# The first stream's matrix memory turned by VectorE blocks and DRAM, in the second stream's written order

## The chip, the cores and the metric

The kernel runs on one core of one Trainium2 chip. The metric is the device time of one execution in microseconds (us). A core has five engines that run their own instruction queues: TensorE (PE; its weight loads are shown as PEld), VectorE (DVE), ScalarE (ACT), GpSimd (POOL) and SyncE (SP), the last of which issues most of the DMAs here.

## The reference

One encoder layer on two independent sequences of 512 tokens and 1024 channels, called stream 0 (the prompt) and stream 1 (the sample). Cut to what matters:

```python
x = x + 0.5 * swiglu(rms_norm(x, ffn1_norm), ...)
h = rms_norm(x, mix_norm)
aq, ak, av, mq, mk, mv, gate_pre, o_pre, g_att, g_mlstm = split(h @ w_in)
att = gqa_block_attention(rope(norm(aq)), rope(norm(ak)), av)         # 8 heads of 64
mem = mlstm_bidirectional(mq, mk, mv, gate_pre, bias, o_pre, head_norm)  # 4 heads of 128
merged = sigmoid(g_att) * (att @ w_up_att) + sigmoid(g_mlstm) * (mem @ w_up_mlstm)
x = x + merged @ w_out
x = x + 0.5 * swiglu(rms_norm(x, ffn2_norm), ...)
```

The matrix memory `mlstm_bidirectional` is written chunk by chunk, forward and backward. It equals, for each head, a 512x512 matrix of scores q·k times exponential weights (a lower triangle for the forward direction, an upper one for the backward direction), each row divided by its own denominator, times the values. Then come an RMS norm over each head, a gain and a sigmoid gate.

## The kernel before

**Tiling.** Activations are held transposed, channels on the 128 partitions and 512 tokens along the free axis, as a pair of float32r tiles: a rounded part (hi, `xh`) and the rest (lo, `xl`). Every weight is split in the same way, on ScalarE (hi, L284) and VectorE (lo, L285), and every product takes three matmuls (hi·hi, hi·lo, lo·hi). Stream 0 reads raw weights from the inputs, splits them and parks both parts in DRAM (L309); stream 1 reads them back (L299).

**Order.** The body is written with a tile framework whose planner puts the instructions of each engine into a queue: it simulates the program, takes the ready instruction of the highest priority (program order, changed by `shifted(n)`), and gives each tile a place in its pool when it is first touched; a place comes free with the last use of its tile. `pin` keeps one instruction behind the one written before it on its engine, and `mark` does so where `marks[0]` is set. So the written order is a preference, and on the chip the queues are fixed.

**Units.** `go` (L792) takes units (load, compute). It calls a unit's load at once and keeps `ahead[0]` units waiting in `held` (1 in stream 0, 2 in stream 1) before it writes their matmuls. In stream 0 the load (`load_w`, L292) reads the raw weights, splits them and parks them. A projection unit has 24 matmuls of 512 columns (8 blocks of 128 channels, three products), an `up_unit` (the merges) 12.

**Pools.** `apool` has seven places of 16 KB a partition (line 31: `bufs=7`, all under one tag): xh, xl, box, kv, qT, mg, att, mem, Vm, mh, ml and others take turns in them. `wpool` has four places `wr` for raw weights and four `w8` for split ones; `t2` has eleven tiles of 128x512 and `f2` four.

**The matrix memory.** `mix(s, ...)` runs for each stream s. After attention it does four heads:

- `mem_head(h)` (L1299): four blocks of scores (L1309, three matmuls each), the exponential weights on ScalarE (L1323), their product with row sums on VectorE (L1325), the denominators (L1329 to L1331), and one row of 512 weights for each 128 queries (L1336 to L1339). The masked rows come from `mem_rows` (L1091), on VectorE in stream 1 and for head 0, on GpSimd for heads 1 to 3 of stream 0.
- In stream 0, `mem_out(h, Ts)` (L1359) turns these 512x512 weights by 16 TensorE transposes of 128x128 (L1372), splits each turned piece from PSUM (L733, L734) and multiplies with the values `Vm` (L1381).
- In stream 1, `mem_blocks` (L1342) turns 32x32 blocks on VectorE (eight instructions a head, L1347) into two `wr` tiles, `mem_send` (L1351) writes them to DRAM with eight DMAs of GpSimd's queue, and `mem_out` reads each piece back whole with a DMA (L1368). The product comes out with its tokens in block order, and a copy (L1387) puts it right.
- Both end with the norm and the gate of the head and a split into `mem[:, h]`.

Other units fill TensorE meanwhile: values, the queries and keys of later heads (`mem_qk`), attention gates, `merge_att` (needs `att`), input gates `mem_gate`. `merge_mem` (L856 into the banks pss and pst) needs all four heads. Stream 1 has its order written out by hand, with sends of one head ahead of the product of the head before (L1401); stream 0 runs a loop of four heads with a queue of fillers (L1423).

Of the kernel before, what the change touches and what calls it, by code (L numbers as in the profile page):

```python
# [16 lines left out]
P = 128  # L17
# [9 lines left out]
def encoder(ctx, tc, I, outs):  # L27
# [91 lines left out]
    def f(ap):  # L119
        return ap.bitcast(F32)  # L120
# [171 lines left out]
    def load_w(view, key, park=True):  # L292


        if key in parked:
            d, shape = parked[key]
            w2 = wpool.tile(shape, F32R, tag="w8", bufs=4, name=nm("w"))
            for i in range(2):
                nc.sync.dma_start(f(w2[:, i]), d[:, i])  # L299
            return w2[:, 0], w2[:, 1]  # L300
        raw = fetch_w(view)
        with shifted(-WEIGHTS):
            hi, lo = split_w(raw, V_)
        if not park:
            return hi, lo
        shape = [P, 2] + list(raw.shape[1:])
        parked[key] = d, _ = dpool.tile(shape, F32, name=nm("wpark")), shape
        for i, t in enumerate((hi, lo)):
            nc.sync.dma_start(d[:, i], f(t))  # L309
        return hi, lo  # L310

# [470 lines left out]
    win_v = w_in.rearrange("(k p) c -> p k c", p=P)  # L782


    held = []
    ahead = [1]
    marks = [False]

    def mark(i, last):
# [1 line left out]

    def go(*units):  # L792
        for load, comp in units:
            held.append((comp, load()))
            while len(held) > ahead[0]:
                c, w = held.pop(0)
                c(w)

    def flush():
        while held:  # L800
            c, w = held.pop(0)
            c(w)

# [61 lines left out]
    def mix(s, xh, xl, early=None, extra=None, after=None):  # L865
# [9 lines left out]
        def F2(dtype=F32):  # L875
            return T2(dtype, "f2")
# [207 lines left out]
        def mem_rows(h, d):  # L1084

            eb = T2(F32, "eb")
            eb3 = eb.rearrange("p (b s) -> p b s", b=4)
            nc.sync.dma_start(eb3, ebuf[d, :, h, :].partition_broadcast(P))
            em = T2(F32, "eb")
            em3 = em.rearrange("p (b s) -> p b s", b=4)  # L1090
            (V_ if s or not h else G_).tensor_tensor(em3, eb3, tabs[3][:, d].unsqueeze(1).to_broadcast([P, 4, P]), op=ALU.add)  # L1091
            return eb3, em3

        def mem_scales():
# [91 lines left out]
        def among(n):  # L1186
            for _ in range(n):
                if not between:
                    if not held:
                        return  # L1190
                    c, w = held.pop(0)
                    if queue:
                        load, c2 = queue.pop(0)
                        held.append((c2, load()))
                    between.extend(c.steps(w))
                between.pop(0)()

# [62 lines left out]
        def up_unit(part, d, src, done, bank=None):  # L1260
            def load():
                if d % 2 == 0:
                    wv = I[("w_up_att", "w_up_mlstm")[part]][0].rearrange("(k p) c -> p k c", p=P)
                    wups[part, d // 2] = load_w(wv[:, :, d * P:(d + 2) * P], ("up", part, d))

            def comp(_):
                wu = wups[part, d // 2]
                cl = slice((d % 2) * P, (d % 2 + 1) * P)
                done(proj_w(wu[0][:, :, cl], wu[1][:, :, cl], lambda k: (src[:, k, 0, :], src[:, k, 1, :]), 4,
                            bank and bank()))  # L1270
            return load, comp

        def merge_att(d):
            def done(pu):
                V_.scalar_tensor_tensor(mg[:, d, :], mg[:, d, :], 1.0, pu, op0=ALU.add, op1=ALU.mult)
            return up_unit(0, d, att, done)
# [64 lines left out]

        def mem_blocks(h, Ts):  # L1342

            q = [wpool.tile([P, 8, 4, 32], F32, tag="wr", bufs=4, name=nm("qt")) for _ in range(2)]
            for i in range(4):
                for g in range(2):
                    V_.transpose(q[g][:, :, i, :],  # L1347
                                 Ts[i][0][:, g * 256:(g + 1) * 256].rearrange("p (n m) -> p n m", m=32))
            return h, q

        def mem_send(h, q):  # L1351

            for g in range(2):
                for a in range(4):
                    mark(nc.gpsimd.dma_start(tbuf[h % 2][8 * g:8 * g + 8, :, a, :].rearrange("n r x -> r n x"),
                                      q[g][32 * a:32 * a + 32].rearrange("r n i m -> r n (i m)")), True)
            return h % 2

        def mem_out(h, Ts):  # L1359
# [32 lines left out]
            turned_ = own[0] if own else F2()  # L1392
            row = block_sums(h2, turned_)
            with shifted(60):
                rh = block_rstd(row, DM)
# [2 lines left out]
                V_.scalar_tensor_tensor(og, og, hn[:, h:h + 1], Rh, op0=ALU.mult, op1=ALU.mult)  # L1398
                split(og, mem[:, h, 0, :], mem[:, h, 1, :])

        if s:  # L1401
            qk2, qk3 = [[mem_qk(h, j) for j in range(2)] for h in (2, 3)]
            ma = [merge_att(d) for d in range(KD)]
            marks[0] = True
            q = mem_blocks(0, mem_head(0))
            at = [mem_send(*q)]
            go(*mem_values(), *qk2)
            q = mem_blocks(1, mem_head(1))
            go(*qk3, ma[0], ma[1])
            mem_out(0, at[0])  # L1410
            at.append(mem_send(*q))
            q = mem_blocks(2, mem_head(2))
            go(att_gate(6), att_gate(7), ma[2], ma[3])
            mem_out(1, at[1])
            at.append(mem_send(*q))
            q = mem_blocks(3, mem_head(3))
            go(*ma[4:])
            mem_out(2, at[2])
            at.append(mem_send(*q))
            go(*[mem_gate(d) for d in range(EARLY)])  # L1420
            mem_out(3, at[3])
            marks[0] = False
        for h in range(HM if not s else 0):  # L1423
            Ts = mem_head(h)
            if h == 0:
                go(*mem_values())
            queue.append(merge_att(2 * h))
            if h == 0:
                queue.append(merge_att(1))
            fill(1 + s)  # L1430
            mem_out(h, Ts)
            if h + 2 < HM:
                queue.extend([att_gate(h + 6), mem_qk(h + 2, 0), mem_qk(h + 2, 1)])
            if h:
                queue.append(merge_att(2 * h + 1))
            fill(99)
# [4 lines left out]
        flush()  # L1441
        yield None


# [551 lines left out]
```

## Time and profile before

| | us |
|---|---|
| median of 3 runs | 2030.96 |
| the runs | 2028.93 to 2032.43 |
| the profiled execution | 2029.24 |
| its span, first to last instruction | 2027.5 |

| stage of the profiled execution | us from the span's start |
|---|---|
| first feed-forward block, both streams | 0 to 649 |
| stream 0: projections and attention | 649 to 811 |
| stream 0: matrix memory, from its first score | 797 to 930 |
| stream 0: merges with memory | 955 to 977 |
| stream 1: projections and attention | 977 to 1185 |
| stream 1: matrix memory | 1168 to 1310 |
| second feed-forward block | 1382 to 2027 |

In the profile's rows an L number is a line of the kernel. A row of groups gives the number of instructions, their busy time, the mean length of one, and the idle time of the engine just before them with what ended it. A row of windows gives, for a stretch of time, the busy time of PE, PEld, DVE, ACT and POOL with the number of instructions, then TensorE's granted clock and the busy share and rate of the DMA engines.

### The profile page before, as it was taken

The page shows a single profiled execution, that of the slowest core. Times are in us where ns is not written, and L with a number is a line of the kernel's source. Part 1 is how long each engine was busy: PE and PEld are TensorE (multiplying, and loading weights), DVE is VectorE, ACT ScalarE, POOL GpSimd, SP SyncE. Part 2 cuts the span into 40 slices and gives each one's busy share as a digit, 9 for nine tenths or more (in the row PEclk, how much of TensorE's full clock was granted, in tenths as well). Part 3 has the DMA queues.
Part 4 walks back from the last instruction along what each step waited for, and adds up shares of the span by engine and source line. Part 5 has one row for each costly group of instructions (what it writes and reads, how often), then busy time and mean ns, then how long its engine had stood idle before and what let it go on. Part 6 is the DMA issues. An engine that isn't in the chain of part 4 may idle for free.

```text
span 2027.5 us, 26874 instructions
## 1 busy us (share of the span) xinstructions
PE 2015.1 (99%) x9129; PEld 1661.4 (82%) x9129; DVE 1592.6 (79%) x2830; ACT 919.2 (45%) x1677; POOL 249.7 (12%) x313
## 2 busy tenths in 40 slices
PE   9999999999999999999999999999999999999998
PEld 7888888888888888788888878888888888888887
DVE  8989898896688788786566867377798988786797
ACT  7644444443224477653325655245444444442224
POOL 0243344201003000100120023011000000000001
PEclk9999999999999999999999999999999999999999
DMA  9778787799766766868657668867565655699753
GB/s 313 233 235 271 228 279 244 258 337 373 264 220 220 274 194 198 267 206 300 210 165 220 205 228 264 274 208 238 157 210 171 226 168 178 204 339 349 272 194 120
DMA packets 329546, 482.11 MB, mean 238 GB/s; under 512 B 23016, under 2 KB 196160, under 8 KB 328128
## 3 DMA queue, kind: packets, MB, share of 16 engines
q1 hardware_dynamic: 316352, 439.27, 64.9%
q0 software_dynamic: 12896, 40.86, 5.9%
q8 instruction: 72, 1.18, 0.2%
q14 instruction: 66, 0.54, 0.1%
q10 hardware_dynamic: 160, 0.27, 0.0%
HBM read 308.70 MB, written 171.61 MB: 237 GB/s over the span
## 4 chain that ended last, share of the span: by engine, by line
PE 94%; DVE 2%; DMA 2%; issue 1%; ACT 1%; SPq 0%; DVEq 0%; ACTq 0%
PE mm L856 16%; PE mm L380 11%; PE pso L380 11%; PE pst L380 11%; PE mm L650 9%; PE mm L842 5%; PE pss L380 5%; PE pss L650 4%; PE pst L650 4%; PE mm L821 3%; PE pso L650 3%; PE pss L1118 1%; PE pso L1165 1%; PE pso L1381 1%; PE pst L856 1%; PE pss L856 1%
## 5 line engine op out<-in xcount | busy, mean ns | idle before, releaser
L380 PE MATMUL pst<-xc,w 128*128 128x512 f32 x1056 | 253.8, 389 | 0.5 <-ACT t L415 0.5
L380 PEld LDWEIGHTS pst<-xc,w 128*128 128x128 f32 x1056 | 198.1, 188 | 42.0 <-ACT t L415 0.9
L380 PE MATMUL mm<-xc,w 128*128 128x512 f32 x972 | 229.8, 390 | 0.8 <-ACT t L388 0.8
L380 PEld LDWEIGHTS mm<-xc,w 128*128 128x128 f32 x972 | 181.8, 188 | 39.5 <-ACT t L388 1.9
L650 PE MATMUL mm<-rt,w 128*128 128x512 f32 x765 | 178.7, 389 | 0.0
L856 PE MATMUL mm<-xh,w 128*128 128x512 f32 x560 | 176.0, 391 | 0.0
L650 PEld LDWEIGHTS mm<-rt,w 128*128 128x128 f32 x765 | 143.5, 188 | 29.8
L338 ACT ACTIVATE w<-t 128x512 fp32r<-128x512 f32 x176 | 107.6, 628 | 130.7 <-issue 59.1
L339 DVE TENSOR_TENSOR w<-t,w 128x512 fp32r<-128x512 f32 x176 | 120.2, 701 | 31.7 <-ACT w L338 30.0
L380 PE MATMUL pso<-xc,f 128*128 128x512 f32 x528 | 127.1, 390 | 0.1
L380 PE MATMUL pss<-xc,w 128*128 128x512 f32 x528 | 126.8, 389 | 0.0
L380 PE MATMUL pso<-xc,w 128*128 128x512 f32 x528 | 126.8, 389 | 0.0
L856 PEld LDWEIGHTS mm<-xh,w 128*128 128x128 f32 x560 | 104.9, 188 | 21.8
L380 PEld LDWEIGHTS pso<-xc,f 128*128 128x128 f32 x528 | 98.9, 188 | 21.5 <-DVE t L419 1.1
L380 PEld LDWEIGHTS pss<-xc,w 128*128 128x128 f32 x528 | 99.1, 188 | 20.6
L380 PEld LDWEIGHTS pso<-xc,w 128*128 128x128 f32 x528 | 99.1, 188 | 20.6
L842 PE MATMUL mm<-xh,w 128*128 128x512 f32 x336 | 110.5, 395 | 0.0
L856 PE MATMUL mm<-xl,w 128*128 128x512 f32 x280 | 109.6, 391 | 0.0
L733 ACT ACTIVATE w<-wr 128x512 fp32r<-128x512 f32 x72 | 45.1, 632 | 138.3 <-PE pso L650 70.6
L733 ACT ACTIVATE w<-t 128x512 fp32r<-128x512 f32 x82 | 51.8, 632 | 107.4 <-PE pst L650 62.4
L650 PE MATMUL pss<-rt,w 128*128 128x512 f32 x396 | 93.7, 389 | 0.0
L650 PE MATMUL pst<-rt,w 128*128 128x512 f32 x396 | 93.7, 389 | 0.0
(464 smaller groups left out, 4168.1 us busy)
## 6 DMA issues: line engine op xcount, KB each, us to landing
rt<-rbuf SPq DMA_DIRECT2D x154, 512.0 KB, 5.8
w<-wpark SPq DMA_DIRECT2D x112, 512.0 KB, 5.1
wpark<-w SPq DMA_DIRECT2D x64, 512.0 KB, 3.6
wr<-in_ffn_w_gate_dram SPq DMA_DIRECT2D x62, 512.0 KB, 5.5
wr<-in_ffn_w_up_dram SPq DMA_DIRECT2D x44, 512.0 KB, 4.8
rbuf<-f SPq DMA_DIRECT2D x86, 256.0 KB, 4.3
rbuf<-R SPq DMA_DIRECT2D x82, 256.0 KB, 4.7
rbuf<-tab SPq DMA_DIRECT2D x74, 256.0 KB, 3.9
```

The source lines that it names most:

```text
L338: pin(nc.scalar.activation(t[:, 0], src, AF.Copy))
L339: pin(V_.tensor_tensor(t[:, 1], src, f(t[:, 0]), op=ALU.subtract))
L380: nc.tensor.matmul(p, a[:, k, :], xt[:, b, k, :], start=(first and k == 0 and i == 0), stop=(k == HK_ - 1 and i == 2), skip_group_check=True)
L650: nc.tensor.matmul(p, u[:, a, d * P:(d + 1) * P], r[:, b, ts], start=(first and q == 0 and k == 0), stop=(q == len(us) - 1 and k == 2), sk ...
L733: nc.scalar.activation(hi, src, AF.Copy)
L821: mark(nc.tensor.matmul(p[b][:, :N], a[:, k, bs], w_[:, kl, :], start=(k == 0 and i == 0), stop=(k == KD - 1 and i == 2)), (kl, b, i) == ( ...
L842: pin(nc.tensor.matmul(p[0], a[:, k, :], b, start=(k == 0 and i == 0), stop=(k == n - 1 and i == 2)))
L856: mark(nc.tensor.matmul(p, a[:, k, :], b, start=(k == 0 and i == 0), stop=last), last)
L1118: pin(nc.tensor.matmul(p, qT[:, h, b * P:(b + 1) * P], kv[:, hk * 2 + j, :], start=(j == 0), stop=(j == 1)))
L1165: pin(nc.tensor.matmul(pos[h], Vst[:, kb, h // 4, :], w, start=(kb == KBS[0] and i == 0), stop=(kb == KBS[3] and i == 1)))
L1381: mark(nc.tensor.matmul(po, vm[:, a, t, hs_], b, start=(t == 0 and n == 0), stop=(t == 3 and n == 2)), True)
```

## The change

Stream 0 takes stream 1's way: its four heads are turned by VectorE blocks and through DRAM, in the same written order. Its block tiles lie in a tile of their own in `apool` (three pairs of block tiles and a row for the sums), not in `wr`. Head 2's queries and keys go to places in `mem` that heads 2 and 3 fill later. All masked rows are added on VectorE. `load_w` now returns a function: the raw read is written at once, the splitting when a unit passes from `fetched` to `held`; in stream 0's memory, two units wait in `fetched` and one in `held`. Six input gates are written ahead of the last head's product.

```diff
 def load_w(view, key, park=True):
         if key in parked:
-            d, shape = parked[key]
...
+            def ready():
+                d, shape = parked[key]
...
+            return ready
         raw = fetch_w(view)
-        with shifted(-WEIGHTS):
-            hi, lo = split_w(raw, V_)
...
+        def ready():
+            with shifted(-WEIGHTS):
+                hi, lo = split_w(raw, V_)
...
+        return ready
...
+    deep, ahead = [0], [1]
     def go(*units):
         for load, comp in units:
-            held.append((comp, load()))
+            fetched.append((comp, load()))
+            while len(fetched) > deep[0]:
+                hold()
             while len(held) > ahead[0]:
                 c, w = held.pop(0)
                 c(w)
+    def hold():
+        c, w = fetched.pop(0)
+        held.append((c, w and w()))
...
         def mem_qk(h, j):
-                if j == 0 and not s:
+                if j == 0 and not s and h != 2:
...
-                elif s:
+                elif s or h == 2:
...
-            (V_ if s or not h else G_).tensor_tensor(em3, eb3, ...)
+            V_.tensor_tensor(em3, eb3, ...)
...
         mem = A([P, HM, 2, S], F32R, "mem")
-        own = [T2(F32, "R")] if s else []
+        if s:
+            own = T2(F32, "R")
+        else:
+            blocks = A([P, 8, S], F32, "broken")
+            broken = blocks[:, 0:6].rearrange("p (q a) (n i m) -> p q (a n) i m", a=2, i=4, m=32)
+            own = blocks[:, 6]
...
+                q = [broken[:, (2 * h + g) % 3] for g in range(2)]
...
-        if s:
-            qk2, qk3 = [[mem_qk(h, j) for j in range(2)] for h in (2, 3)]
+        qk2, qk3 = [[mem_qk(h, j) for j in range(2)] for h in (2, 3)]
+        ma = [merge_att(d) for d in range(KD)]
+        deep[0] = 0 if s else 2
+        marks[0] = True
+        q = mem_blocks(0, mem_head(0))
+        at = [mem_send(*q)]
+        go(*mem_values(), *qk2)
+        q = mem_blocks(1, mem_head(1))
+        go(*qk3, ma[0], ma[1])
+        mem_out(0, at[0])
+        at.append(mem_send(*q))
+        q = mem_blocks(2, mem_head(2))
+        go(att_gate(6), att_gate(7), ma[2], ma[3])
+        mem_out(1, at[1])
...
+        go(*[mem_gate(d) for d in range(EARLY)])
+        mem_out(3, at[3])
+        marks[0] = False
-        for h in range(HM if not s else 0):
-            Ts = mem_head(h)
-            if h == 0:
-                go(*mem_values())
...
-            mem_out(h, Ts)
...
-        go(*[mem_gate(d) for d in range(EARLY * s, KD)])
+        go(*[mem_gate(d) for d in range(EARLY, KD)])
```

More of the change, by code (lines that the diff above doesn't have):

```diff
@@ L295, in load_w @@
         if key in parked:
-            d, shape = parked[key]
[L297 to L300, printed above, removed]
-        raw = fetch_w(view)
-        with shifted(-WEIGHTS):
-            hi, lo = split_w(raw, V_)
-        if not park:
-            return hi, lo
[L306 to L310, printed above, removed]
+            def ready():
+                d, shape = parked[key]
+                w2 = wpool.tile(shape, F32R, tag="w8", bufs=4, name=nm("w"))
+                for i in range(2):
+                    nc.sync.dma_start(f(w2[:, i]), d[:, i])
+                return w2[:, 0], w2[:, 1]
+            return ready
+        raw = fetch_w(view)
+        def ready():
+            with shifted(-WEIGHTS):
+                hi, lo = split_w(raw, V_)
+            if park:
+                shape = [P, 2] + list(raw.shape[1:])
+                parked[key] = d, _ = dpool.tile(shape, F32, name=nm("wpark")), shape
+                for i, t in enumerate((hi, lo)):
+                    nc.sync.dma_start(d[:, i], f(t))
+            return hi, lo
+        return ready
     V_ = nc.vector
@@ L782, in encoder @@
     win_v = w_in.rearrange("(k p) c -> p k c", p=P)
-    held = []
-    ahead = [1]
+    fetched, held = [], []
+    deep, ahead = [0], [1]
     marks = [False]
@@ L797, in go @@
                 c(w)
+    def hold():
+        c, w = fetched.pop(0)
+        held.append((c, w and w()))
     def flush():
-        while held:
+        while fetched or held:
+            if fetched:
+                hold()
             c, w = held.pop(0)
@@ L1090, in mem_rows @@
             em3 = em.rearrange("p (b s) -> p b s", b=4)
-            (V_ if s or not h else G_).tensor_tensor(em3, eb3, tabs[3][:, d].unsqueeze(1).to_broadcast([P, 4, P]), op=ALU.add)
+            V_.tensor_tensor(em3, eb3, tabs[3][:, d].unsqueeze(1).to_broadcast([P, 4, P]), op=ALU.add)
             return eb3, em3
@@ L1193, in among @@
                         load, c2 = queue.pop(0)
-                        held.append((c2, load()))
+                        fetched.append((c2, load()))
+                        hold()
                     between.extend(c.steps(w))
@@ L1263, in load @@
                     wv = I[("w_up_att", "w_up_mlstm")[part]][0].rearrange("(k p) c -> p k c", p=P)
-                    wups[part, d // 2] = load_w(wv[:, :, d * P:(d + 2) * P], ("up", part, d))
+                    ready = load_w(wv[:, :, d * P:(d + 2) * P], ("up", part, d))
+                    return lambda: wups.update({(part, d // 2): ready()})
             def comp(_):
@@ L1342, in mem_blocks @@
         def mem_blocks(h, Ts):
-            q = [wpool.tile([P, 8, 4, 32], F32, tag="wr", bufs=4, name=nm("qt")) for _ in range(2)]
+            if s:
+                q = [wpool.tile([P, 8, 4, 32], F32, tag="wr", bufs=4, name=nm("qt")) for _ in range(2)]
+            else:
+                q = [broken[:, (2 * h + g) % 3] for g in range(2)]
             for i in range(4):
@@ L1391, in mem_out @@
             V_.scalar_tensor_tensor(og, og, 1.0, po, op0=ALU.add, op1=ALU.mult)
-            turned_ = own[0] if own else F2()
+            turned_ = own
             row = block_sums(h2, turned_)
```

35 lines of the change are left out of this document (6 added, 29 removed).

## The prediction

> **What bounds the kernel now.** I read the page first: how full TensorE is.
>
> ```profile
> span 2027.5 us, 26874 instructions
> ...
> PE 2015.1 (99%) x9129; PEld 1661.4 (82%) x9129; DVE 1592.6 (79%) x2830; ACT 919.2 (45%) x1677; POOL 249.7 (12%) x313
> ```
>
> TensorE is busy for 2015.1 of 2027.5 us. Only two things can change the time by much: matmuls that are removed, and waits that are added to TensorE's queue. Next come the windows around the first matrix memory (stream 0): from the first score of head 0 to the first merge with memory (797 to 955), its dense part, the part with gates only, the merges, and the dense part of the second matrix memory, which already runs as the change wants it.
>
> ```profile
> core 0: us, PE busy (x) PEld busy (x) DVE busy (x) ACT busy (x) POOL busy (x), PEclk, DMA share, GB/s
> 797.00:955.00 158.00, 156.90 (x728) 127.06 (x727) 118.76 (x267) 87.50 (x178) 8.66 (x7) 1.00 0.76 255
> ...
> 811.00:906.00 95.00, 93.90 (x434) 75.61 (x433) 74.70 (x182) 58.68 (x133) 8.21 (x6) 1.00 0.71 233
> 906.00:955.00 49.00, 49.00 (x226) 40.39 (x225) 34.13 (x72) 19.06 (x28) 0.00 (x0) 1.00 0.93 322
> 955.00:985.00 30.00, 30.00 (x162) 26.00 (x161) 24.76 (x32) 11.20 (x18) 8.07 (x6) 1.00 0.58 191
> ...
> 1182.00:1268.00 86.00, 85.38 (x374) 69.06 (x373) 65.49 (x205) 46.92 (x123) 25.14 (x44) 1.00 0.79 265
> ```
>
> TensorE lacks 1.1 us of 158, at full clock (1.00). VectorE does 118.76 us of work there, 75%, ScalarE 87.50. So the stage is TensorE's, and VectorE is the next candidate. Then the chain of waits, cut to the last head and what follows it.
>
> ```profile
> 828.50 0.87 PE pst L1372 x8
> ...
> 917.65 0.91 PE mm L856 x4
> 918.56 0.91 PE pso L1381 x4
> 919.47 2.95 PE mm L856 x13
> 922.41 0.27 PE pst L238 x2
> 922.68 32.55 PE mm L856 x143
> 955.23 2.72 PE pss L856 x12
> ```
>
> The chain runs on TensorE almost everywhere. Eight of the transposes that the change removes (L1372) hold it for 0.87 us, 0.109 each; a matmul costs 32.55/143 = 0.228. After the last head's product (L1381) come 32.55 us of input gates alone, and only then the merges (L856 into pss and pst), the first work that needs the finished memory. That stretch is the cover of everything the change makes later.
>
> **What is removed.** All of head 0 to 3's turns on TensorE:
>
> ```profile
> L1372 PE MATMUL pst<-ident,t x64: 270/272/328, 828.3 to 916.2; 128*128 128x128 f32 x64
> ```
>
> The 270 ns are the pipelined length; what the queue gains is the spacing of 0.109. 64 x 0.109 = **7.0 us** off TensorE, all on the path since TensorE has no other slack. This is the one sure term. The two PSUM banks they used come free too, which I price at nothing: in this stretch no transpose waits for a bank long enough to matter (1.1 us idle in all).
>
> [...]
>
> **What is added on VectorE.** The block turns and the moved additions have rows:
>
> ```profile
> L1347 DVE STREAM_TRANSPOSE qt<-t x32: 407/411/444, 1191.0 to 1261.9; 128x256 f32<-128x256 f32 x32
> ...
> L1091 DVE TENSOR_TENSOR box<-box,tab x10: 653/690/1370, 712.4 to 1237.4; 128x512 f32<-128x512 f32 x10
> ...
> L1091 POOL TENSOR_TENSOR box<-box,tab x6: 1285/1294/1734, 819.3 to 880.6; 128x512 f32<-128x512 f32 x6
> ```
>
> 32 turns x 0.411 = 13.2 us, and six mask additions that leave POOL, 6 x 0.690 = 4.1: VectorE gains 17.3 us. The split of each turned piece now reads SBUF in place of PSUM at the same length (not counted). ScalarE gains four copies of 0.6 us. VectorE then has 118.8 + 17.3 = 136 us to do in 158 - 7 = 151, 90%; the dense windows before ran at 79% and 76%. While TensorE still has gates to run, that costs nothing. If the cover is gone, each us that the last head is late is a us of the time.
>
> **What is added on the queues.** Per head, POOL issues eight sends and four fetches, which its queue runs in the written order, so a send that waits for a turn holds the fetches of the head before it.
>
> ```profile
> L1355 POOL DMA_DIRECT2D tbuf<-qt x32: 582/585/618, 1194.2 to 1266.3; - x32
> ...
> DMA to landing us min/median/max: 3.8/5.9/7.1
> ...
> L1368 POOL DMA_DIRECT2D f<-tbuf x16: 537/546/572, 1203.0 to 1272.6; - x16
> ```
>
> 4 x (8 x 0.585 + 4 x 0.546) = 27.5 us of POOL's queue in 150: hidden, since POOL did 8.66 us there and loses the additions. Nobody else waits for POOL before the merges' splits. SP's queue loses nothing and gains nothing in number; its raw weight reads go out earlier. The transfers add 8 x 0.25 MB on engines that are 76% busy: below noticing.
>
> **What becomes late.** A head now goes out to DRAM and back. Five rows show the length: in stream 0 the last head (reciprocal of its denominators, last split into mem), in stream 1 the reciprocals of heads 2 and 3, the copies of their products out of PSUM, and the last split into mem.
>
> ```profile
> 910.22 0.20 DVE L1331 RECIPROCAL dn<-dn 128x8 f32<-128x8 f32 x1
> 929.64 0.69 DVE L734 TENSOR_TENSOR mem<-box,mem 128x512 fp32r<-128x512 f32 x1
> ...
> L1331 DVE RECIPROCAL dn<-dn x2: 195/196/196, 1237.3 to 1257.5; 128x8 f32<-128x8 f32 x2
> ...
> L1387 ACT ACTIVATE t<-pso x2: 598/600/601, 1267.8 to 1297.1; 128x512 f32<-128x512 f32 x2
> ...
> 1308.92 0.69 DVE L734 TENSOR_TENSOR mem<-box,mem 128x512 fp32r<-128x512 f32 x1 [0.70 <-ACT mem L733]
> ```
>
> Now: 910.22 to 930.33, 20.1 us. With the trip: head 2 takes 1237.3 to 1267.8, 30.5, from reciprocal to copy (head 3 takes longer, queued behind gates), and head 3 takes 1297.1 to 1309.6, 12.5, from copy to mem: 43 us, which is 23 more. The cover: mem is ready at 930.33 and needed at 955.07, 24.7 us; 7.0 of it go because TensorE arrives earlier: 17.7. But the merges take head 3 last, nine of twelve matmuls of each need heads 0 to 2 only, and four banks (two PSs, two PTs) can hold such starts: 4 x 9 x 0.228 = 8.2. Cover 25.9 against 23, and VectorE's extra 17.3 us lies partly ahead of the last head: the two are near each other. I put **2.0 us** of waiting on TensorE, nearer to none than to much because the planner fills a wait of one unit with another, as it does in stream 1, whose dense window misses 0.6 us of 86. The ends: minus 2.3 (the dense part's own waits go, since the raw weights are there earlier: two 10 us windows below hold 40 and 42 matmuls where 46 fit, ten missing at 0.228) and plus 15 (below).
>
> ```profile
> 810.00:820.00 10.00, 9.29 (x40) 6.80 (x39) 8.01 (x24) 9.95 (x26) 0.74 (x1) 1.00 0.29 106
> ...
> 850.00:860.00 10.00, 9.60 (x42) 7.36 (x40) 9.64 (x29) 4.41 (x7) 3.00 (x2) 1.00 0.67 241
> ...
> 950.00:960.00 10.00, 10.00 (x46) 8.29 (x45) 5.05 (x6) 3.61 (x6) 0.00 (x0) 1.00 0.72 267
> ```
>
> Head 2's queries and keys leave the w8 tiles and the turned sums leave f2 tiles: places come free, priced at nothing. Six gates now stand ahead of the last head in the written order, as in stream 1, and their results hold six of the eleven t2 tiles that the heads use too; that can only delay the heads, and stands in the second case below.
>
> The read-ahead itself I price at nothing: ScalarE is at 9.95 of 10 in the first of these windows and VectorE at 9.64 of 10 in the second, so what was missing there was an engine and not a weight.
>
> **Sum.** -7.0 + 2.0 = -5.0 us. The profiled execution took 2029.24 us (its span and 1.74 around it), the median of the runs shown is 2030.96; I take the difference to the median: **2026.0 us**, -0.25%. 0.2%, 4.1 us, is about what a measurement can tell from no change.
>
> **Rivals.**
> *Given back.* VectorE at 90% keeps heads 2 and 3 later than the latency alone: if half of its 17.3 us falls ahead of the last head, the delay is 23 + 8.6 = 31.6 against 25.9, a wait of 5.7, and the sum is -1.3: 2029.7. For it: 79% is the densest that this stage ran. Against it: windows such as 850 to 860 show VectorE at 96%, and the gates' stretch, where VectorE has 15 us of 49 free, now takes the last two heads. [...]
> *An eighth tile for seven places (slower).* apool holds seven big tiles (line 31). From the end of attention box, xh, xl, mg and att are held; the change wants the block tile, Vm and mem beside them, so the one of the three that is first touched last gets its place only when att is given up, after the last attention merge. I take mem for that one: stream 0's head 2 now keeps its queries and keys there, so head 2 can't begin its scores before.
>
> ```profile
> L1275 DVE SCALAR_TENSOR_TENSOR mg<-mg,mm x3: 680/681/689, 899.7 to 909.5; 128x512 f32<-128x512 f32 x3
> ...
> L1309 PE MATMUL pss<-mem x12: 389/389/389, 1225.6 to 1231.6; 128*128 128x512 f32 x12
> ```
>
> att's last merge ends at 909.5. Without the 48 transposes of heads 0 to 2 (5.2) and the 36 matmuls of head 2's scores and product and head 3's scores (8.2) ahead of it, that is 896. From head 2's first score in stream 1 (1225.6) to head 3's reciprocal (1257.5) pass 31.9, then 43: 75 us, mem ready at 971. TensorE runs out at 955 - 7 + 8.2 = 956: a wait of 15, sum +8: **2039**. It decides only if att is given up after 956 - 75 = 881. For it: the count of tiles. Against it: the planner may run the attention merges ahead of other units, and stream 1 took its 75 us without being pressed.
> *Without effect.* That the turns don't leave TensorE can't be: the line is no longer called.
>
> **How the numbers follow.** Forecast 0.43, own range 2021 to 2027. Given back 0.27, 2027 to 2035. Eighth tile 0.30, 2035 to 2041. Faster by over 0.2% is the first case, within it the second, slower the third: 0.43, 0.27, 0.30. Low end: -7.0 - 2.3 and 1.7 for the spread of the runs (2028.93 to 2032.43), 2020; high end: 2039 and 1.5, 2040.5. It is no narrower since two cases of other signs hold more than half.
>
> **What would show it.** Right: no L1372, 64 matmuls fewer, VectorE near 136 us between the first score and the first merge, and the merges about 5 us earlier with under 3 us of TensorE idle in the stage. Given back: TensorE waiting ahead of the merges for VectorE's last split into mem. Eighth tile: head 2's scores not before the last attention merge, and ScalarE's first write into mem right behind it. The forecast is wrong too if the wait sits inside the dense part (scores behind L1325, projections behind L285), since then VectorE bounds it and the cover at the end does not count.

## The result, and the profile after

The changed kernel took 2055.37 us (median of 4 runs, 2052.36 to 2057.26) against 2029.95 (2027.05 to 2032.43) for the kernel before: 25.4 us more, a ratio of 1.0124 (95% interval 1.0105 to 1.0144). The prediction said 2026.0, with 2020 to 2040.5 as its range.

The page of the changed kernel, its span, the busy times and the DMA totals:

```profile
span 2055.5 us, 26873 instructions
...
PE 2016.6 (98%) x9065; PEld 1657.1 (81%) x9065; DVE 1605.3 (78%) x2868; ACT 922.5 (45%) x1681; POOL 271.8 (13%) x355
...
DMA packets 332362, 490.49 MB, mean 239 GB/s; under 512 B 23784, under 2 KB 196928, under 8 KB 330944
```

64 matmuls are gone (9129 to 9065), and yet PE was busy 1.5 us longer (2015.1 before). Its idle time went from 2027.5 - 2015.1 = 12.4 us to 2055.5 - 2016.6 = 38.9. So the lost time has two parts: 26.5 us more of waiting, and matmuls that took longer. These cost the 7.0 us that the removed transposes would have given and 1.5 more, 8.5 in all. The windows of the changed kernel (columns as in the prediction) show where:

```profile
core 0: us, PE busy (x) PEld busy (x) DVE busy (x) ACT busy (x) POOL busy (x), PEclk, DMA share, GB/s
797.00:955.00 158.00, 132.79 (x542) 101.95 (x541) 109.12 (x260) 79.18 (x166) 26.68 (x47) 0.92 0.81 258
811.00:906.00 95.00, 81.42 (x329) 62.83 (x329) 64.41 (x149) 48.77 (x108) 13.68 (x24) 0.95 0.86 275
...
930.00:940.00 10.00, 2.78 (x13) 1.97 (x11) 7.03 (x21) 3.46 (x6) 3.29 (x6) 0.83 1.01 305
940.00:950.00 10.00, 5.77 (x12) 2.70 (x12) 3.94 (x6) 3.15 (x6) 3.83 (x8) 0.67 1.05 352
950.00:960.00 10.00, 9.82 (x37) 8.09 (x38) 7.21 (x20) 4.11 (x7) 1.94 (x4) 0.82 0.93 310
```

Nearly all of the waiting is in stream 0's matrix memory: TensorE lacks 25.2 us of 158 where it lacked 1.1. Half of that is in the dense part (13.6 of 95), where the DMA engines' share rose from 0.71 to 0.86, and the hole at 930 to 950 follows it. VectorE did 109 us, fewer than the 118.76 before in the same stretch: it was held up with the rest. Two tiles name the first cause. The rows of `mem` and of `att` in the changed kernel, with first and last start; the row ending in "4.4, 1" says what released `mem`'s writer:

```profile
L868 PE MATMUL pss<-mem,w x48: 389/389/389, 983.4 to 1002.2; 128*128 128x512 f32 x48
...
L1328 PE MATMUL pss<-mem x12: 389/389/497, 912.0 to 916.4; 128*128 128x512 f32 x12
...
L738 DVE TENSOR_TENSOR mem<-box,mem x4: 684/684/685, 912.6 to 980.9; 128x512 fp32r<-128x512 f32 x4
L737 ACT ACTIVATE mem<-f x2: 615/624/634, 910.8 to 911.3; 128x512 fp32r<-128x512 f32 x2
...
  PE mm L868: 4.4, 1
```

```profile
L868 PE MATMUL mm<-att,w x96: 387/389/628, 862.6 to 910.3; 128*128 128x512 f32 x96
```

The last attention merge starts its last matmul at 910.3. ScalarE, which had waited 4.4 us for exactly that, writes into `mem` at 910.8, and head 2's scores (L1328) start at 912.0, right behind its queries. The merges with memory (L868 into pss) start at 983.4, some 71 us after head 2's first score; before, they began at 955.07. The chain that ended last, from head 2's scores on:

```profile
912.09 0.61 PE pss L1328 x2
...
923.03 1.67 DVE broken L1369 x5
...
924.98 4.05 POOL tbuf L1377 x7
929.04 8.28 DMA tbuf<-broken
...
937.88 0.53 POOL f L1390
938.40 7.42 DMA f<-tbuf
...
945.90 0.64 ACT t L737
946.59 1.53 PE pso L1403 x3
...
950.18 3.91 PE mm L868 x9
...
971.46 12.13 PE mm L868 x53
983.60 1.59 PE pss L868 x7
```

Where the chain ran on TensorE before, it now runs over turns, POOL's sends and two transfers of 8.28 and 7.42 us. TensorE's longest waits stand beside it (engine, line, what it waited for, sum, times, longest):

```profile
PE pso L1403 <- ACT t L737: 13.1, 7, 7.3
PE pso L1403 <- DVE t L738: 4.4, 1, 4.4
```

Both are products (L1403) that wait for a piece to be split, and the two have unlike causes. The 7.3 us stand ahead of head 2's product, up to 940.1, and ScalarE's split had itself waited for the piece to come back from DRAM. The 4.4 us stand ahead of head 1's product. There ScalarE had split its part by 882.5, but VectorE stood for 5.4 us, until 883.3, waiting for the read of a masked row (L1103), and the other part of the split was behind that row in its queue.

In the same way the input gates stand behind head 2's product in TensorE's queue: it waits, and then some 28 us of gates run between 950 and 983. `mem` is complete at 981.6 (the last split, L738, starts at 980.9), so TensorE never waits ahead of the merges.

### The profile page after: what moved, and what is told of

It reads as the page before. It is cut to its first block, busy times and chain, and to the rows that moved or that the text cites. A ratio compares the mean times of both kernels' runs of the same rounds, so it can differ in the third digit from the quotient of the medians.

```text
span 2055.5 us, 26873 instructions
## 1 busy us (share of the span) xinstructions
PE 2016.6 (98%) x9065; PEld 1657.1 (81%) x9065; DVE 1605.3 (78%) x2868; ACT 922.5 (45%) x1681; POOL 271.8 (13%) x355
## 2 busy tenths in 40 slices
DMA packets 332362, 490.49 MB, mean 239 GB/s; under 512 B 23784, under 2 KB 196928, under 8 KB 330944
## 4 chain that ended last, share of the span: by engine, by line
PE 89%; DMA 5%; DVE 2%; ACT 2%; issue 1%; SPq 1%; POOL 0%; DVEq 0%; POOLq 0%; ACTq 0%
PE mm L868 13%; PE pso L384 12%; PE pst L384 11%; PE mm L384 10%; PE mm L654 8%; PE pss L384 6%; PE mm L854 5%; PE pss L654 4%; PE pst L654 4%; PE pso L654 3%; PE mm L833 3%; PE pss L1130 1%; PE pso L1177 1%; DMA f<-tbuf 1%; PE pst L868 1%
## 5 line engine op out<-in xcount | busy, mean ns | idle before, releaser
L868 PE MATMUL mm<-xh,w 128*128 128x512 f32 x560 | 180.4, 397 | 5.7 <-DVE Vm L897 3.6
L868 PEld LDWEIGHTS mm<-xh,w 128*128 128x128 f32 x560 | 107.0, 191 | 29.3 <-DVE Vm L897 4.0
L868 PE MATMUL mm<-xl,w 128*128 128x512 f32 x280 | 110.9, 396 | 0.0
L854 PE MATMUL mm<-xh,w 128*128 128x512 f32 x336 | 110.5, 395 | 0.0
```

What stands on the lines that cost most here:

```text
L854: pin(nc.tensor.matmul(p[0], a[:, k, :], b, start=(k == 0 and i == 0), stop=(k == n - 1 and i == 2)))
L868: mark(nc.tensor.matmul(p, a[:, k, :], b, start=(k == 0 and i == 0), stop=last), last)
```

## The experiments

Differences are to the runs of the kernel before on the same chip, medians in us; each carries an interval of about ±3 us, and what lies between two variants one of 3 to 5. Diffs are against the changed kernel unless said, and cut to the lines that matter. Every variant is planned anew, so its queues can differ in more than the edit.

**The place of `mem`.** Two kernels free head 2 of it in unlike ways, and a third takes a rival cause away. `e1_qk2_w8` puts head 2's queries and keys of stream 0 back into a `w8` tile:

```diff
-                if j == 0 and not s and h != 2:
+                if j == 0 and not s:
...
-                elif s or h == 2:
+                elif s:
```

> Stream 0's head 2 keeps its queries and keys in a w8 tile, as before the change; all else as after. Place theory (mem is the eighth tile for seven places: it is first written at 911, right behind the last attention merge, and until then head 2's two scaled projections sit in two of the four f2 tiles, through which the pieces of heads 0 and 1 are read back): the read-backs of heads 0 and 1 follow each other without the 22 us and 14 us gaps, head 2's scores start well before 900, and the time falls from 2055 to 2030-2040. Trip theory (products stand in TensorE's queue ahead of other work and wait for the DRAM trip whatever the places do) and VectorE theory (17 us more work than the stage can take): 2050-2057.

Measured: 2038.53, +9.8 (1.005, 1.0035 to 1.0065).

```profile
L1328 PE MATMUL pss<-qk x48: 387/389/507, 799.6 to 899.9; 128*128 128x512 f32 x48
```

```profile
L868 PE MATMUL mm<-att,w x96: 388/389/478, 871.0 to 913.5; 128*128 128x512 f32 x96
```

```profile
L868 PE MATMUL pss<-mem,w x48: 389/389/389, 967.7 to 986.5; 128*128 128x512 f32 x48
```

The rows of its scores, of `att` and of `mem`: all heads' scores now end ahead of the last attention merge, `att` goes as late as in the changed kernel (913.5), and the merges start 15.7 us earlier.

`e16_att_unread` keeps head 2 in `mem` and lets stream 0's attention merges read other blocks, so it leaves attention's result out:

```diff
-                done(proj_w(..., lambda k: (src[:, k, 0, :], src[:, k, 1, :]), 4,
+                done(proj_w(..., (lambda k: (xh[:, k, :], xl[:, k, :])) if src is att and not s else
+                            (lambda k: (src[:, k, 0, :], src[:, k, 1, :])), 4,
```

> After, but in stream 0 the merges with attention read the first four blocks of xh and xl in place of att, so attention's result is left out of the sum: the same matmuls, and att's place is free at the end of attention, near 814, in place of 911. Place theory: mem is written by 870, head 2's scores start near 860, the merges with memory start 25 us or more earlier than after's 983.6 and the time is 2025-2038. DMA theory (the trips and raw reads are slow since the DMA engines are full with parking): 2048-2057, head 2 early but the waits in other places.

Measured: 2038.42, +9.4 (1.0047, 1.0032 to 1.0062). Its rows of `mem`:

```profile
L868 PE MATMUL pss<-mem,w x48: 389/389/389, 965.9 to 984.7; 128*128 128x512 f32 x48
...
L1329 PE MATMUL pss<-mem x12: 387/390/398, 854.8 to 869.2; 128*128 128x512 f32 x12
```

Head 2's scores, still from `mem`, start 57 us earlier, and the time is that of `e1`. So it is `att`'s late release that holds head 2, and nothing else about keeping its queries in `mem`.

`e5_fetch_t2` reads the pieces back into `t2` tiles, in case the four `f2` places were what the fetches wait for:

```diff
-                    p = F2()
+                    p = F2() if s else T2()
```

> In stream 0 the turned pieces are read back into t2 tiles in place of f2 tiles; mem still waits for att's place. Place theory, by its part in the f2 tiles alone: TensorE's waits for heads 0 and 1 (about 15 us of those between 855 and 900) mostly go, heads 2 and 3 still begin at about 900-911 and keep their 12 us of waiting near 930-950: 2038-2047. Trip theory: 2050-2057. VectorE theory: 2052-2057.

Measured: 2056.22, +27.5 (1.013, 1.0113 to 1.0147), no different from the changed kernel. Head 2's scores start at 909.8, against 912.0. Combined with `e1` (`e15_w8_t2`) the same edit did not gain either:

> e1 with the turned pieces read back into t2 tiles in place of f2 tiles. In e1 GpSimd waited 26.6 us for f2 tiles held by queries and keys. If that holds TensorE up: 4-10 us less than e1's 2038.5, 2029-2035. If t2 tiles are the scarcer: 2038-2046.

Measured: 2042.14, +13.1 (1.0062, 1.0045 to 1.0079). The gain of 8 us or more that the account of the place expected by its part in the `f2` tiles did not come. `f2`'s places are not the bound.

**Freeing `att` earlier by the written order.** `e3_ma_first` writes the eight attention merges right behind the values, and four input gates later on. In it attention gates 6 and 7 stand behind the merges that use them, so two of the eight blocks are merged without their own gate; `e3b_ma_first` has those gates first and five input gates later:

```diff
-        go(*mem_values(), *qk2)
...
+            go(*mem_values(), att_gate(6), att_gate(7), *ma)
...
-        go(*qk3, ma[0], ma[1])
...
+            go(*qk2, *qk3, mem_gate(0))
```

> Stream 0's written order alone is changed: the eight attention merges come right behind the values, head 2's and 3's queries and keys behind them, and four of the six input gates fill the later gaps. Place theory: att is given up near 855 in place of 911, mem gets its place there, the time falls to 2028-2040. Trip theory: the products still wait for the trips, 2045-2057. VectorE theory: the same work in another order, 2050-2057.

> The written order of e3 with attention gates 6 and 7 ahead of the attention merges that use them, and five of the six input gates in the later gaps. Place theory: att is given up near 865, mem gets its place there, heads 2 and 3 and the merges follow some 40-50 us earlier than in after: 2030-2038. Trip and VectorE theories: 2045-2057.

Measured: 2033.05, +4.3 (1.0018, 1.0009 to 1.0027), and 2043.8, +14.6 (1.0073, 1.0058 to 1.0088). In `e3b` the last attention merge ends at 865, 45 us earlier than in the changed kernel, and head 2 starts earlier too:

```profile
L1328 PE MATMUL pss<-mem x12: 389/512/792, 880.4 to 894.9; 128*128 128x512 f32 x12
```

`e3b` gains 10.8 of the 15.6 us that `e1` gains, and missed its range (2030 to 2038). What of `e3`'s further 10 us comes from merges that need not wait for two gates was not separated. The order has a price of its own: TensorE then stands 4.6 us at a gate in one piece (L868 behind L901), where the changed kernel loses 2.1. What holds that gate I only argue (the `t2` places). Two more on top of `e3b` missed too: with head 2 in `w8` besides (`e12_ma_first_w8`), and with the masked rows of heads 1 to 3 on GpSimd again (`e9_ma_first_pool`).

> e3b's order (attention merges first, att given up near 865) with head 2's queries and keys in a w8 tile as in e1. If the two gains add where they are separate: 2030-2038. If the place is the one cause that both cure: 2036-2044.

> As e3b, with the masked rows of heads 1 to 3 added on GpSimd again, 6 x 0.69 = 4.1 us less for VectorE. VectorE theory for what is left over before: 2-4 us less than e3b. Weight theory (TensorE waits for raw weights and their splitting): no change against e3b within 1.5 us.

Measured: 2046.82, +18.0 (1.0095, 1.0078 to 1.0111), and 2049.15, +20.0 (1.0095, 1.008 to 1.011). The first gains nothing once `att` goes early (3.4 us more than `e3b`, with intervals that overlap), which fits the place as the one cause that both remove, but it lies above the range of either account. The second is 5.4 us slower than `e3b`: GpSimd's queue is the worse place for those rows there. Why was not isolated.

**The DRAM trip.** `e17_w8_notrip` is `e1` without it: pieces are split straight from the block tiles. `e18_after_notrip` is the changed kernel without it. `e20_w8_traffic` is `e17` with the same sends, and read-backs that go from DRAM to another place in DRAM, while nobody waits for the data. All three leave out the joining of the 32x32 blocks into whole rows.

```diff
-            for g in range(2):
+            for g in range(2 if s else 0):
...
-                if j < 4 and moved:
+                if j < 4 and moved and not s:
+                    p = halves[h][j // 2][:, j % 2 * 4:j % 2 * 4 + 4].rearrange("p n i m -> p (n i m)")
+                elif j < 4 and moved:
```

> e1 (head 2's queries and keys in a w8 tile) without the trip to DRAM in stream 0: the pieces are split straight from the block tiles in SBUF, so sends, read-backs and the joining of the 32x32 blocks into whole rows are left out; the turns, splits and products stay. Trip theory for the 10 us that e1 leaves over before: 2022-2029, products no longer wait. VectorE theory: 2035-2040.

> After without the trip to DRAM in stream 0, as in e17. Place theory: head 2 still begins behind att's last merge near 905, so most of that wait stays: 2036-2046, and e17 is 8 us or more faster. Trip theory alone: about the time of e17.

> e17 (2029) with the traffic of the trips put back and nothing waiting for its data: each head's blocks are sent to DRAM as in e1, and the pieces are read from there into a spare buffer in DRAM, while the products still take their pieces straight from the block tiles, so the joined rows stay left out. Traffic theory (the added bytes slow raw reads, parking and mask rows): 2034-2039, near e1's 2038.5. Waiting theory (what costs is the product standing in TensorE's queue until its piece has come): 2027-2032.

Measured: `e17` 2029.05, +0.2 (1.0001, 0.9992 to 1.0011); `e18` 2044.09, +15.3 (1.0076, 1.0061 to 1.0091); `e20` 2036.21, +7.6 (1.0037, 1.0022 to 1.0052). With the changed kernel and `e1` this is a square:

| | with the trip | without |
|---|---|---|
| head 2 in `mem` | +25.4 | +15.3 |
| head 2 in `w8` | +9.8 | +0.2 |

The place costs 15.6 with the trip and 15.1 without; the trip costs 10.1 with the place and 9.6 without. They add up. In `e18` the place is the whole rest: its rows of `mem` show head 2 still at the end of the attention merges (its last one starts at 892.1).

```profile
L868 PE MATMUL pss<-mem,w x48: 389/389/389, 967.9 to 986.8; 128*128 128x512 f32 x48
...
L1328 PE MATMUL pss<-mem x12: 387/391/497, 893.8 to 898.9; 128*128 128x512 f32 x12
```

`e20` splits the trip: its traffic alone costs 7.4 of the 9.6, give or take 4, and waiting for the data some 2.2, which this interval does not tell from nothing. The raw weight reads (L277, 797 to 985, from issue to landing) come later with the traffic; before, after, `e17` and `e20` in this order:

```profile
DMA to landing us min/median/max: 5.1/6.1/7.6
```

```profile
DMA to landing us min/median/max: 4.5/7.6/14.8
```

```profile
DMA to landing us min/median/max: 4.6/5.9/8.1
```

```profile
DMA to landing us min/median/max: 4.3/8.0/16.3
```

The longest lands after 16.3 us against 8.1. So do the reads of the masked rows (L1100), in `e17` and then in `e20`:

```profile
DMA to landing us min/median/max: 3.5/4.5/6.0
```

```profile
DMA to landing us min/median/max: 3.2/4.8/15.6
```

In `e20`, which waits for no piece, one long wait of TensorE is new, and VectorE waits for masked rows:

```profile
DVE box L1103 <- DMA box<-ebuf: 10.4, 3, 8.9
...
PE mm L868 <- DVE w L285: 7.6, 1, 7.6
```

The two are one event. TensorE waits for a split weight, up to 853.8, but not because its raw read was late: ScalarE had split its part of that weight by 844.3. VectorE stood for 8.9 us, until 850.7, waiting for the read of a masked row, and its part of the split (L285) was behind that row in its queue. In `e1` the same event is smaller: 3.9 us of VectorE, 2.7 of TensorE. So the link from this traffic to TensorE that the rows show is a late masked row in VectorE's queue. In the kernel before, VectorE adds only head 0's masked rows and GpSimd waits for the others (76.2 us in five waits). Reading these rows earlier was not tried. The write in `e20` goes to DRAM where the kernel's goes to SBUF, so 7.4 is the traffic's price only as far as the two weigh alike. `e13_after_nopark` and `e14_w8_nopark` go the other way: split weights of stream 0's memory aren't parked (stream 1 reads and splits them again, and pays for it, so their totals say nothing here).

```diff
-            if park:
+            if deep[0]:
+                loose.add(key)
+            elif park and key not in loose:
```

> After, but the weights split in stream 0's memory aren't parked in DRAM; stream 1 reads these raw and splits them again, which it pays for itself, so the start of stream 0's merges is to be compared and the total only loosely. DMA theory: raw reads and tbuf trips land 1-3 us sooner each, the merges with memory start 8 us or more before after's 983.6. Place theory: att's last merge still ends near 905-910 and the merges start within 5 us of 983.6.

> e1 (head 2's queries and keys in a w8 tile, merges from 967.8) without the parking in stream 0's memory, as in e13. DMA theory for what e1 leaves over before (10 us): the merges start at 955-960. VectorE and place theories: within 4 us of 967.8.

Measured: 2115.34 and 2097.13; what counts is the start of the merges, 972.9 against 983.4 and 956.3 against 967.7, 10.5 and 11.4 us earlier. Not all of that is traffic: a parked weight also holds its `w8` tile until the write is done, for which ScalarE waits 3.3 us in `e1`. `e13`'s windows and its raw reads:

```profile
797.00:955.00 158.00, 138.02 (x581) 107.41 (x580) 115.75 (x275) 82.39 (x171) 27.35 (x48) 0.96 0.47 140
```

```profile
DMA to landing us min/median/max: 3.2/3.7/8.1
```

At a DMA share of 0.47 reads land in 3.7 us, and the place is still waited for (head 2's scores at 909.3). `e19_before_trips`, the kernel before with sends and read-backs added, was meant to price the traffic there:

```diff
+            if not moved:
+                for i in range(4):
+                    for a in range(4):
+                        nc.gpsimd.dma_start(tbuf[h % 2][...], Ts[i][0][...])
+                for j in range(4):
+                    nc.gpsimd.dma_start(F2(), tbuf[h % 2][...])
```

> Before, and in stream 0 each head's weights are also sent to DRAM by GpSimd's queue and read back into f2 tiles that nobody reads: the traffic of the trips (16 smaller sends a head in place of 8) with nothing waiting for its data. DMA theory, that the traffic itself slows raw reads and parking enough to stop TensorE: 5-12 us over before, 2034-2041. Otherwise, that only waiting for the trip costs: within 3 us of before.

Measured: 2044.59, +15.8 (1.008, 1.0065 to 1.0095), but not for the traffic alone. Its waits:

```profile
DVE f L225 <- DMA f<-tbuf: 14.3, 3, 6.3
PE pst L238 <- DVE row L232: 13.4, 3, 5.1
```

TensorE's 13.4 us stand behind an `f2` place that an added read-back holds. It decides nothing.

**The turns.** `e8_turns_twice` is the kernel before with each of the 64 transposes done twice; `e10_turn_twice` the changed kernel with each block turn of stream 0 done twice; `e21_w8_fewturns` is `e17` with only 8 of the 32 turns, so it also leaves three quarters of the turned weights out:

```diff
-                    for i in range(4):
+                    for i in (0, 1, 2, 3) * 2:
```

```diff
-            for i in range(4):
+            for i in (0, 1, 2, 3) if s else (0, 0, 1, 1, 2, 2, 3, 3):
```

```diff
-            for i in range(4):
+            for i in range(0 if s else 3, 4):
```

> Before, with each of the 64 transposes on TensorE done twice: the price of the term that the change removes. By the chain's 0.109 us each: 7.0 us more than before, 2035-2038 (before 2029). If the transposes hide behind other waits: under 3 us more.

> After, with each block turn of stream 0 done twice: VectorE gets 32 x 0.41 = 13.2 us more. Place theory: the end is set by att's last merge and the two heads behind it, so only the turns of the heads near TensorE's waits count: 0 to 8 us more, 2055-2063. VectorE theory: the stage is VectorE's, so the whole 13 us appear or more: 2066-2072.

> e17 with the last of each head's four pairs of block turns alone (24 of 32 turns, 9.9 us of VectorE, are left out with what they would move; the block tile is cleared once). VectorE theory for the 7 us that e17 should gain by its missing transposes and does not: 2020-2025. If VectorE's load does not matter: within 2 us of e17's 2029.

Measured: `e8` 2036.77, +7.6 (1.0032, 1.0018 to 1.0046); `e10` 2060.12, +30.9 (1.015, 1.0135 to 1.0165), an interval that still overlaps the changed kernel's; `e21` 2023.58, -5.0 (0.9974, 0.9964 to 0.9983), apart from `e17`. The windows of `e17`, then of `e21`:

```profile
797.00:955.00 158.00, 150.76 (x656) 121.18 (x655) 127.77 (x306) 91.37 (x186) 1.06 (x2) 0.98 0.75 248
811.00:906.00 95.00, 87.76 (x368) 69.76 (x368) 83.69 (x227) 62.74 (x140) 0.00 (x0) 0.96 0.77 251
```

```profile
797.00:955.00 158.00, 155.41 (x687) 124.96 (x686) 125.84 (x285) 92.06 (x186) 1.05 (x3) 1.00 0.77 261
811.00:906.00 95.00, 93.22 (x409) 75.19 (x408) 86.11 (x222) 65.80 (x145) 0.00 (x0) 1.00 0.83 275
```

With all turns VectorE is busy 88% of the dense part and TensorE lacks 7.2 us of 95; with 24 fewer (24 x 0.406 = 9.7 us of VectorE) TensorE lacks 1.8 and the end comes 5.2 us earlier. VectorE's share does not fall by it (91%), since more other work fits into the same stretch; what goes are waits behind the turns. The longest of TensorE in that stretch, in `e17` and then in `e21`:

```profile
PE mm L868 <- ACT t L737: 3.4, 1, 3.4
```

```profile
PE mm L868 <- DVE f L1056: 1.4, 1, 1.4
```

The 3.4 us of `e17` end at 872.6, right after VectorE has run eight turns (869.1 to 871.8).

**The read-ahead.** `e2_deep0` turns it off:

```diff
-        deep[0] = 0 if s else 2
+        deep[0] = 0
```

> No read-ahead of raw weights in stream 0's memory (deep 0), all else as after. If the read-ahead is what hurts (reads and splits in another order, wr tiles held), the time falls by 5 us or more, to under 2050. If it helps, TensorE waits more for weights and the time is over 2058. Place theory: neither matters much, 2052-2058.

Measured: 2060.73, +32.0 (1.0157, 1.0142 to 1.0172), some 6 us above the changed kernel's +25.4; the intervals just touch. The read-ahead helps rather than harms.

No kernel here that does the whole computation takes less time than the one before. Block tiles in other places, and more `f2` places, weren't tried.

## Why the prediction failed, step by step

The runs give this sum, each step the difference of two kernels:

| step | from | us |
|---|---|---|
| 64 transposes gone | the prediction's 7.0 (`e8` doubles them: 7.6) | -7.0 |
| 8 turns, the new order and the rest | `e21`, -5.0 | +2.0 |
| 24 more turns on VectorE | `e17` - `e21` | +5.2 |
| the trip's traffic | `e20` - `e17` | +7.4 |
| waiting for the pieces | `e1` - `e20` | +2.2 |
| `mem` waits for `att`'s place | after - `e1` | +15.6 |
| sum | | +25.4 |

The sum closes by its making, since each step ends at a kernel where another begins; the second row is what is left over. The 2.0 and the 2.2 are within the noise.

- **"64 x 0.109 = 7.0 us"**: right. Done twice (`e8`), the transposes cost 7.6 more. Even without the trip, VectorE's turns only come out even (`e17`, +0.2).
- **VectorE's 17.3 us "costs nothing" while TensorE still has gates**: wrong. 9.7 us of turns cost 5.2, in the dense part, where TensorE waits for what VectorE's queue holds behind the turns. That is the wait "inside the dense part" which the prediction named as a sign against itself. *Given back* has the same engine, but its wait is ahead of the merges, for the last split into `mem`, and no run shows that one; that its 2029.7 is near the 2029.05 of `e17` is luck.
- **"six mask additions that leave POOL, 6 x 0.690 = 4.1"**: right for the additions, but VectorE's queue now also waits for the reads of these rows, which the sum has at nothing: 12.9 us in the changed kernel, 10.4 in `e20`, 1.7 in `e17`, which has no trip.
- **"The transfers add 8 x 0.25 MB ... below noticing"**: the term that was mis-sized. A head's weights are 512 x 512 x 4 bytes, 1.05 MB, each way: 8.4 MB, as the page says (490.49 - 482.11, the total before). That is four times the traffic, on engines that were 76% busy, and it cost 7.4 us (`e20` - `e17`).
- **"I put 2.0 us of waiting on TensorE ... because the planner fills a wait of one unit with another"**: wrong, in size and in place. TensorE waited 26.5 us more. The prediction set the gates against a late head, up to the merges; but the queues are fixed, and head 2's product waited up to 940.1 with some 28 us of gates behind it. The gates behind that product covered nothing of its 7.3 us of waiting. Whether the written order without `mark` would have let them pass was not tried.
- **The read-ahead at nothing, since "what was missing there was an engine and not a weight"**: read off the kernel before, whose raw reads landed in 6.1 us. With the trip they land later (7.6), and without the read-ahead the kernel is slower by some 6 us (`e2`), with intervals that just touch.
- **POOL's 27.5 us**: right in size (32 x 0.582 + 16 x 0.546 = 27.4); what its order alone costs was not isolated.
- **An eighth tile for seven places**: this came, with both signs it was given. That its wait of 15 us is so near the measured 15.6 is luck: it had TensorE run out of gates at 956 and wait for `mem` until 971. In fact `mem` was complete at 981.6 and the gates lasted until 983.4; the time is lost at the products, for which TensorE waits 17.5 us here and 2.5 in `e1`. Too low were its weight, 0.30, and its total. Against it stood that the planner may run the merges earlier (it didn't: 910.3 against an estimate of 896) and that stream 1 took its 75 us unpressed (70 here, 912.0 to 981.6). For it stood a count of tiles, which the code settles: seven places, eight tiles, and head 2's first instruction behind the eighth.

The step that failed is thus the +2.0 of waiting, which set the gates as a cover against everything that comes late. Late came three things, at different places of the stage: head 2, held by `att`'s place (15.6); reads behind the trip's traffic (7.4); and work behind VectorE's turns (5.2). The cases were priced as if one of them would come. They came together, so the time lay 16 us above the dearest single case, 2039. The premise that only removed matmuls and added waits can change the time left out a third term, matmuls that ran slower behind some of the waits (7.9 us against `e17`, in the last section).

## What to carry to other kernels

Count the tiles against the places of a pool at the moment a new one is touched, and ask what is queued behind its first write: a place can be waited for too, and here that cost 15.6 of 25.4 us. Work out a transfer's bytes from its shape, and price it through the reads beside it and through the queues that stand behind these reads: here, on DMA engines that were 76% busy before, the median raw read landed after 8.0 us with the traffic (`e20`) and 5.9 without (`e17`). Before counting work as cover for a wait, look whether it is ahead of the waiting instruction in the queue: here some 28 us of gates stood behind a product that waited 7.3. Rivals at different places of the stage added up here (the place 15.6 with the trip and 15.1 without); the range must reach to their sum.

## What was not expected of the hardware

Some waits of TensorE cost more than their length here. In 940 to 950 the granted clock was 0.67, and the matmuls right behind the 7.31 us wait ran slower: six took 3.03 us, where six of the same shape took 1.52 at 869.76. The timeline of PE in the changed kernel (start, length, line, idle time before it in brackets):

```profile
940.09 3.03 PE L1403 MATMUL pso<-t,Vm 128*128 128x512 f32 x6 [7.31 <-ACT t L737]
...
951.20 1.06 PE L868 MATMUL mm<-xh,w 128*128 128x512 f32 x2
...
954.62 0.62 PE L868 MATMUL mm<-xh,w 128*128 128x512 f32 x2
```

A pair takes 1.06 us at 951 and 0.62 at 954.6. Over the whole kernel the same 9065 matmuls kept PE busy for 2016.6 us here and for 2008.7 in `e17`:

```profile
PE 2008.7 (99%) x9065; PEld 1655.2 (82%) x9065; DVE 1604.5 (79%) x2868; ACT 922.0 (45%) x1681; POOL 237.0 (12%) x307
```

So 7.9 of the 26.1 us between the two spans (2055.5 and 2029.4) is slower matmuls, and 18.2 is waiting. The length of a wait did not by itself tell whether slow matmuls followed: in `e3_ma_first` pairs of 1.05 us came from 872.6 on, 2.1 us after a wait of 2.19 us (up to 870.5), and in `e1` a wait of 2.70 us (up to 851.1) was followed by pairs of 0.62. What decides it was not isolated. In the changed kernel the full rate came back some 3.5 us after the restart at 950.18; the granted clock was 0.64 in 950 to 955 and 1.00 in 955 to 960.
